# An encoder block in Strassen's form: product 1 of four gate groups by a second level, two groups at a time

## The chip, the cores and the metric

The kernel runs on one core of one Trainium2 chip. The metric is the device time of one execution in microseconds, the median of the runs; less is better. PE is the matrix engine, DVE the vector engine, ACT the scalar engine, POOL the GpSimd engine; SP issues the loads.

## The reference, cut to what matters

One layer on 1024 tokens of width 1024, all in float32:

```python
u = rms_norm(x, norm1_g)
q, k, v, cb, cc, ch, ga, gb = jnp.split(u @ w_in, split_pts, axis=-1)
...
y_a = neighbourhood_attention(q, k, v, rpb) @ w_attn_branch
y_b = short_gated_conv(cb, cc, ch, conv_w) @ w_conv_branch
merged = jax.nn.sigmoid(ga) * y_a + jax.nn.sigmoid(gb) * y_b
x = x + merged @ w_o
h = rms_norm(x, norm2_g) @ w_mlp_in
x = x + jnp.square(jax.nn.relu(h)) @ w_mlp_out
```

The change concerns `ga` and `gb`: 1024 tokens times 1024 inputs times 2 x 1024 gate columns of `w_in`.

## The kernel before

**Precision.** A float32 operand is scaled by a power of two and split into two float16 halves, high and low. A product takes three passes (high by high, low by high, high by low), so a product over 512 inputs, 128 output channels and 512 tokens is 4 x 3 = 12 matmuls of 512 columns.

**The gate stage.** Eight groups n = 0 to 7 follow one another. A group takes 128 channels of `ga` and the same of `gb`, and with the two halves of the inputs its weights are a matrix of 2 x 2 blocks (`ch.r`). It is computed by Strassen's scheme in Winograd's form, with seven products in place of eight: `SEVEN` gives for each product the form of the activations (0 to 6) and the form of the weights. Forms 0 to 3 of the activations are quarters or sums that lie in `UT`, 4 and 5 in space of `QD`, 6 in `s4T`; they are made once for all groups. Product 1 is the first quarter of the activations (inputs 0 to 511, tokens 0 to 511) by the first block of the weights, unsummed. `gate_units` (L1349) runs the products in the order 1, 6, 2, 4, 5, 7, 3 and joins them in the tile `sg` (two buffers in turn) by "posts" on DVE and ACT: product 1 is copied to `z[0]`, products 6 and 2 are added to it, `post7` and `post3` give the rest and the sigmoid. Then `branch_units` (L1463) runs four products of the attention's and the convolution's branch (two halves of the tokens each), whose posts multiply by the gates (L1489) and add (L1491) to `m`; `m_done` takes the largest value of `m` (L1344) and splits it into `mH` and `mL` (L1338, L1340).

**Preparing a group.** `prep_s(n + 1)` runs in the background of group n: `rows_scaled` multiplies the rows of the loaded weights by norm 1's gains (ACT, L1260), `forms_sum` squares them (ACT, L1269) and makes the four sums (POOL, L1274) in `gsum`, `sum_of` adds up the squares (L1240, L1241), `scale_of` sums over the partitions by a one-column matmul with `ones` (L201, in `all_sum`) and makes the scale from it in small DVE steps (L204, L435 to L442), and `forms_split` writes the float16 halves `w_s`, ACT the high one (L1294) and DVE the low one (L1290). The branch weights A and B are prepared by `Chunk.prep`: `largest` (L320 to L331), `all_sum`, `pow2`, split (L309 on ACT, L300 on DVE).

**The order.** The program's order is that of one Python run, and each engine takes its instructions in that order. A `unit` issues the matmuls of one product, then lets each generator in `hooks` make one step unless `hold` is set, then issues the posts of the product before it (`settle`), and then `steps` steps of the foreground (`fg`, that is `m_done`) in turn with `ticks` steps of the background (`bg`). A tick goes to the first generator of the background that isn't waiting. Generators wait by `apart` for a number of units, or of columns of matmul (`work`; 6144 is one product). `hold` is set while `w_s` is split. From group 1 on, `norms1` in `hooks` loads pieces of W1, into spare rows of `mH` and `mL` and a tile of its own, and sums their squares on ACT (L1386).

**PSUM.** Eight buffers of 512 columns, three of kind "d", three "s", two "o"; `anybank` goes round over the kinds as "dsodsods". The products, the branch halves and the one-column sums of the background all take theirs there. A new use of a buffer waits for the last reader of the old one.

In the MLP the same second level is in use before the change (`deep1`, `quarters`, `slices`): there, in groups 6 to 13, product 1 of two groups is done by seven smaller products; `w_d` are its weights, `quarter` and `a_d` its sums of the activations, `zt` its partial results.

## Time and profile before

| | us |
|---|---|
| median of 3 runs | 1194.14 (1193.83 to 1194.72) |
| the profiled execution | 1194.58 |
| its span in the trace | 1192.6 |
| PE busy in the span | 1185.4 |
| DVE busy | 959.0 |
| ACT busy | 769.3 |
| POOL busy | 410.5 |

The profiled execution took 2.0 us more than its span; these lie around what the trace shows. The gate stage runs from 297.6 us (product 1 of group 0) to 526.9 us, when the output projection begins. Times in rows are microseconds from the start of the span; a row of a timeline gives start, duration, engine, line, operation, output and inputs with their shapes, the count, and in brackets the idle time before it and what ended it. Matmuls overlap and their ends are modelled, so that the distance of two starts says more than a duration. Rows of a tile or line give the shortest, the median and the longest duration in ns.

### The profile page before, as it was taken

To read this page: it belongs to the slowest core of one execution; us is meant where nothing else is said; L and a number is where in the kernel's file an instruction comes from. 1 tells how busy PE (TensorE), PEld (TensorE's weight loads), DVE (VectorE), ACT (ScalarE), POOL (GpSimd) and SP (SyncE) were. 2 spreads that over 40 slices of the span, in tenths; PEclk is the share of its full clock that TensorE was granted. 3 is DMA by queue.
4 is the path that set the end of the run, shared out by engine and by line. 5 is a ranking of instruction groups with operands and counts; after the bars stand their busy time and mean duration, and the time that the engine had idled before them with its cause. 6 is when DMAs were issued, how large, how long until landed. Compare 5 with 4: busy or idle time off the path is not lost.

```text
span 1192.6 us, 17069 instructions
## 1 busy us (share of the span) xinstructions
PE 1185.4 (99%) x6291; PEld 581.3 (49%) x6291; DVE 959.0 (80%) x1666; ACT 769.3 (65%) x1192; POOL 410.5 (34%) x284
## 2 busy tenths in 40 slices
...
PEclk9999999999999999999999999999999999999999
...
GB/s 296 212 154 214 112 127 134 141 153 113 179 103 179 142 177 144 86 154 130 78 164 150 158 177 176 195 130 133 207 255 203 376 74 264 89 141 194 106 36 106
DMA packets 181283, 189.61 MB, mean 159 GB/s; under 512 B 138192, under 2 KB 138704, under 8 KB 177104
## 3 DMA queue, kind: packets, MB, share of 16 engines
...
## 4 chain that ended last, share of the span: by engine, by line
PE 57%; issue 6%; POOL 5%; DMA 3%; DVE 3%; ACT 2%; SPq 0%; POOLq 0%; DVEq 0%; ACTq 0%
PE ps_s L210 21%; PE ps_d L210 20%; PE ps_o L210 15%; DMA hs<-as 3%; POOL tsum L1671 3%; POOL as L1559 2%; PE ps_d L1158 1%; DVE w L1290 1%; DVE as L2009 1%; SPq L1149 0%; ACT raw L1662 0%; DMA raw<-in_weights 0%; PE ps_o L1122 0%; ACT as L1932 0%; DVE w_s L1290 0%
## 5 line engine op out<-in xcount | busy, mean ns | idle before, releaser
L210 PEld LDWEIGHTS <-ops 128*128 128x128 f16 x1356 | 132.5, 98 | 157.3
L210 PEld LDWEIGHTS <-w 128*128 128x128 f16 x1272 | 124.4, 98 | 127.1 <-issue 0.2
L1158 PE MATMUL ps_d<-uT,w_ws 128*128 128x512 f16 x528 | 123.7, 379 | 0.0
L210 PE MATMUL ps_d<-ops 128*128 128x512 f16 (+1 forms) x528 | 119.7, 377 | 0.0
L1559 POOL TENSOR_TENSOR as<-as 128x512 f32<-128x512 f32 x56 | 92.0, 1643 | 74.0 <-ACT as L1934 71.0
L210 PE MATMUL ps_s<-ops 128*128 128x512 f16 (+1 forms) x516 | 117.1, 377 | 0.0
L2186 ACT ACTIVATE ops<-hf,sc 128x2048 f16<-128x2048 f32 x26 | 52.0, 2000 | 86.0 <-PE ps_d L210 37.5
L210 PEld LDWEIGHTS <-w_s 128*128 128x128 f16 x672 | 65.1, 98 | 79.2 <-DVE w_s L1290 1.5
L210 PEld LDWEIGHTS <-uT 128*128 128x128 f16 x528 | 51.4, 98 | 62.4 <-issue 0.6
L1671 POOL TENSOR_TENSOR tsum<-raw 128x512 f32<-128x512 f32 x28 | 40.5, 1462 | 114.4 <-ACT raw L1662 114.4
L1158 PEld LDWEIGHTS <-w_ws 128*128 128x128 f16 x528 | 51.4, 98 | 54.2
L2188 DVE SCALAR_TENSOR_TENSOR ops<-hf,sc,ops 128x2048 f16<-128x2048 f32 x26 | 69.5, 2673 | 3.5 <-ACT ops L2186 3.5
L210 PE MATMUL ps_o<-ops 128*128 128x512 f16 x312 | 71.6, 379 | 0.0
L1274 POOL TENSOR_TENSOR gsum<-raw 128x512 f32<-128x512 f32 x14 | 18.6, 1341 | 125.4 <-ACT raw L1260 100.0
L210 PE MATMUL ps_d<-u2T,w 128*128 128x512 f16 (+1 forms) x276 | 58.2, 360 | 0.0
L1290 DVE SCALAR_TENSOR_TENSOR w<-tsum,sc,w 128x1024 f16<-128x1024 f32 x28 | 46.3, 1661 | 14.5 <-ACT w L1294 14.5
L210 PE MATMUL ps_s<-u2T,w 128*128 128x512 f16 (+1 forms) x252 | 54.0, 364 | 0.0
L1290 DVE SCALAR_TENSOR_TENSOR w<-raw,sc,w 128x1024 f16<-128x1024 f32 (+1 forms) x20 | 28.2, 1417 | 31.7 <-ACT w L1294 31.7
L1932 ACT ACTIVATE as<-as 128x2048 f32<-128x2048 f32 (+1 forms) x18 | 30.9, 1718 | 31.5 <-DVE as L2009 19.3
L1088 ACT ACTIVATE sz<-sz,sc 128x384 f32<-128x384 f32 (+1 forms) x64 | 37.2, 581 | 20.9 <-DVE sc L1079 13.7
L309 ACT ACTIVATE w_ws<-raw,sc 128x512 f16<-128x512 f32 (+1 forms) x64 | 37.2, 655 | 19.6 <-DVE sc L282 19.6
L210 PE MATMUL ps_s<-u2x,w 128*128 128x512 f16 (+1 forms) x228 | 48.5, 362 | 0.0
...
## 6 DMA issues: line engine op xcount, KB each, us to landing
...
```

The costliest lines, as they stand in the source:

```text
L210: T.matmul(ps, l, r, start=a, stop=b, skip_group_check=free)
L309: A.activation(self.parts[:, 0, f + o:f + o + m], self.raw[p][:, o:o + m], AF.Copy, scale=sc[:, c:c + 1])
L1088: A.activation(z, z, AF.Exp, scale=-1.0, bias=sc[:, d["mx"]], accum_out=sc[:, d["sm"]])
L1158: T.matmul(ps, l, r, start=a, stop=b)
L1274: G.tensor_tensor(t[:, o], a, b, op=OP.add)
L1290: V.scalar_tensor_tensor(o(1), w, sc[:, s], o(0), op0=OP.mult, op1=OP.subtract)
L1559: sub.tensor_tensor(z[o], z[a], z[b], op=op)
L1671: G.tensor_tensor(t[:, o], a, b, op=OP.add)
L1932: A.activation(v[:, 0:4], v[:, 0:4], AF.Relu)
L2009: add, less = (lambda o, a, b, op=op: V.tensor_tensor(o, a, b, op=op) for op in (OP.add, OP.subtract))
L2186: A.activation(P[:, 1, 0], hf, AF.Copy, scale=sc[:, Rs])
L2188: V.scalar_tensor_tensor(P[:, 1, 1], hf, sc[:, Rs], P[:, 1, 0], op0=OP.mult, op1=OP.subtract)
```

## The change

For the groups 2 and 3, and 4 and 5, product 1 of both is computed together: one product over 512 inputs, 2 x 128 channels and 512 tokens, seen as 2 x 2 blocks once more, becomes seven products over 256 inputs, 128 channels and 256 tokens (6 matmuls of 256 columns each). They run in three turns ("slices") of three, two and two products in front of and between the other six products of groups 2 and 4, into three buffers of PSUM that are kept over the turns; the second and third turn add to what the first has left there. The results for both groups go to `z[0]` of their tiles, and groups 3 and 5 begin with product 6.

- `quarters1`, a hook from group 0 on, makes the sums of the activations' first quarter on DVE and splits them (ACT, DVE) into spare rows of `mH` and `mL`.
- For each pair, group n's preparation also loads the first block of group n+1 (256 KB), scales and squares it, and makes the scales of both in one go; then four sums of 256 columns on DVE and five small pieces give the weights of the small products. The first block of the usual seven pieces is left out for both groups.
- The small products have a scale of their own, so products 6 and 2 are joined to them with a factor (`joined`).
- In groups 2 and 4, product 7's post is issued with product 3's; the order there is 5, 4, 7, 6, 2, 3 with the turns in between.
- Ticks: 9 per product in groups 2 and 4 and none at the turns, 6 in the other groups (before: 4, in group 7: 6), 3 per branch unit (before: 4).

```diff
@@ -253,7 +253,7 @@
...
-            self.split = False
+            self.split, self.q = False, None
...
@@ -1262,18 +1262,27 @@
 
     def forms_sum(ch, t, gap):
 
-        sm = cols_of("prep", 2)
+        pair = ch in cS.values() and ch is not cS[0] and ch in [cS[i] for i in PAIRS]
+        sm = cols_of("prep", 4 if pair else 2)
         for i in range(2):
             while len(ch.raw) <= i:
                 yield WAIT
...
+        if pair:
+            yield from pair_square([i for i in PAIRS if cS[i] is ch][0], sm)
         ch.r = [ch.raw[i].rearrange("p (n m) -> p n m", n=2) for i in range(2)]
         (w11, w12), (w21, w22) = ([r[:, 0], r[:, 1]] for r in ch.r)
         for o, a, b in ((0, w11, w12), (1, w12, w22), (2, t[:, 0], w22), (3, t[:, 2], w21)):
             G.tensor_tensor(t[:, o], a, b, op=OP.add)
         yield from apart(work[0], gap * 6144, work)
-        ch.sum = sum_of(sm)
+        if pair:
+            b, a = cols_of("prep", 2), ones[:, 132:134]
+            V.tensor_reduce(sc[:, b], sc[:, sm].rearrange("p (a b) -> p a b", a=2), axis=AX, op=OP.add)
+            V.tensor_copy(a, sc[:, b])
+            ch.sum = a, work[0]
+        else:
+            ch.sum = sum_of(sm)
         yield
 
     last_low = [-9]
@@ -1297,34 +1306,132 @@
 
     def forms_split(ch, t, s, P):
 
+        m = int(ch.q is not None)
+
         def then(n):
-            if n == 1 and ch is not c1[0]:
+            if n == 1 - m and ch is not c1[0]:
                 done[0] += 2
                 load_upto(done[0] + 5)
         r = ch.r
-        todo = [(0, 1, r[0][:, 0:1]), (1, 3, r[1]), (3, 5, t[:, 0:2]), (5, 7, t[:, 2:4])]
+        todo = [(0, 1, r[0][:, 0:1]), (1, 3, r[1]), (3, 5, t[:, 0:2]), (5, 7, t[:, 2:4])][m:]
         yield from parts([((lambda i, a=a, b=b: P[:, a:b, i]), w) for a, b, w in todo], s, then)
+
+    PAIRS = (2,4,)
+    gates, began, a16, sliced = {}, {}, [], set()
+
+    pieces_q = {}
+
+    def form_q(n):
+        v = [r.rearrange("p i (f c) -> p f i c", f=2) for r in pieces_q[n]]
+        return lambda a, b: v[a // 2][:, a % 2:a % 2 + b - a]
+
+    def quarters1():
+
+        z = [v.bitcast(F32) for v in (M[1][:, 1], M[1][:, 2], M[1][:, 3], M[0][:, 1], M[0][:, 2])]
+        rows4 = [v.rearrange("p (s k c) -> p s k c", s=2, k=2) for v in (M[0][:, 4], M[0][:, 5], M[1][:, 4], M[1][:, 5])]
+        for t in range(2):
+            for h in range(2):
+                hi, lo = (UT[:, i, 2 * h:2 * h + 2, 256 * t:256 * t + 256] for i in range(2))
+                V.tensor_tensor(z[2 * t + h].rearrange("p (k c) -> p k c", k=2), hi, lo, op=OP.add)
+                yield
+        for o, a, b, op in ((4, 0, 2, OP.subtract), (2, 2, 3, OP.subtract), (0, 2, 0, OP.subtract), (1, 1, 0, OP.add)):
+            V.tensor_tensor(z[o], z[a], z[b], op=op)
+            yield
+        prev = None
+        for f, i in enumerate((2, 0, 4, 1, None)):
+            if prev:
+                V.tensor_tensor(prev[1], prev[2], prev[0], op=OP.subtract)
+            if i is not None:
+                hi, lo = (rows4[f][:, w].rearrange("p k c -> p (k c)") for w in range(2))
+                A.activation(hi, z[i], AF.Copy)
+                prev = hi, lo, z[i]
+            yield
+        a16.extend(rows4)
+
+    def pair_load(n):
+
+        while n - 1 not in began or units[0] < began[n - 1] + 2:
+            yield WAIT
+        gates[n] = w3p.tile([128, 4, 512], F32, name="sg")
+        SP.dma_start(gates[n][:, 1], bass.AP(tensor=weights.tensor, offset=weights.offset + cS[n + 1].offs[0],
+                                             ap=[[1024, 128], [1, 512]]))
+
+    def pair_square(n, sm):
+
+        sg, ch = gates[n], cS[n]
+        for k in range(4):
+            v = sg[:, 1, 128 * k:128 * k + 128]
+            A.activation(v, v, AF.Copy, scale=sc[:, at(g1, 4 * 0 + k)])
+        for i, v in enumerate((sg[:, 1], ch.raw[0][:, 0:512])):
+            A.activation(sg[:, 2], v, AF.Square, accum_out=sc[:, at(sm, 2 + i)])
+        yield
+
+    def two_scales(am, n):
+
+        a, mark = am
+        yield from apart(mark, n * 6144, work)
+        b, s, inv = cols_of("prep", 2), cols_of("prep", 2), keep(2)
+        bk = anybank()
+        T.matmul(bk[:, 0:2], ones[:, 0:128], a, start=True, stop=True)
+        yield
+        V.tensor_scalar(sc[:, b], bk[:, 0:2], 1e-36, None, op0=OP.max)
+        yield
+        yield from pow2_half(b, 14, s, inv, 9)
+        return s, inv
+
+    def pair_split(n, s):
+
+        ch, sg, W = cS[n], gates[n], form_q(n)
+        x, y = ch.raw[0][:, 0:512], sg[:, 1]
+        d = sg[:, 2:4].rearrange("p a (h c) -> p (a h) c", h=2)
+        b11, b21, b12, b22 = x[:, :256], x[:, 256:], y[:, :256], y[:, 256:]
+        for o, a, b in ((0, b11, b12), (1, b12, b22), (2, d[:, 0], b22), (3, d[:, 2], b21)):
+            V.tensor_tensor(d[:, o], a, b, op=OP.add)
+        yield
+        two = lambda v: v.rearrange("p (h c) -> p h c", c=256)
+        yield from parts([((lambda i, a=a, b=b: W(a, b)[:, :, i]), w) for a, b, w in
+                          ((0, 2, two(x)), (2, 3, two(b22)), (3, 4, d[:, 0:1]), (4, 6, d[:, 1:3]), (6, 7, d[:, 3:4]))],
+                         s, lambda m: None)
+
+    def ratio(s, inv):
+        r = cols_of("prep", 1)
+        V.scalar_tensor_tensor(sc[:, r], sc[:, s], 2.0 ** 9, sc[:, inv], op0=OP.mult, op1=OP.mult)
+        return r
 
     def prep_s(n):
 
         ch = cS[n]
         t = w3p.tile([128, 4, 512], F32, name="gsum", bufs=1)
+        if n in PAIRS:
+            yield from pair_load(n)
         yield from rows_scaled(ch, g1)
-        yield from forms_sum(ch, t, 2 - 0 * (n != 3))
-        s, ch.inv = yield from scale_of(ch.sum, 9, 2 + 1*(n != 3), 0)
+        if n in PAIRS:
+            pass
+        yield from forms_sum(ch, t, (1+(n==2)) if n in PAIRS else 2)
+        s, ch.inv = yield from two_scales(ch.sum, 3) if n in PAIRS else scale_of(ch.sum, 9, 2 if n == 3 else 3, 0)
         hold[0] = True
-        while done[0] < ch.first:
+        while done[0] < ch.first or n - 1 in PAIRS and n - 1 not in sliced:
             yield WAIT
-        ch.P = wsp.tile([128, 7, 2, 512], F16, name="w16_s", tag="ws")
+        ch.P = wsp.tile([128, 8, 2, 512], F16, name="w16_s", tag="ws")
+        if n in PAIRS:
+            P, O = ch.P, cS[n - 1].P
+            pieces_q[n] = P[:, 0], P[:, 7], O[:, 7] if n == 2 else O[:, 0], M[0][:, 3].rearrange(
+                "p (i m) -> p i m", i=2) if n == 2 else O[:, 7]
+            yield from pair_split(n, at(s, 1))
+            ch.q, s, ch.inv = at(ch.inv, 1), at(s, 0), at(ch.inv, 0)
+        elif n - 1 in PAIRS:
+            ch.q = cS[n - 1].q
+        if ch.q:
+            ch.ratio = ratio(s, ch.q)
         yield from forms_split(ch, t, s, ch.P)
         ch.split = True
         hold[0] = False
 
     SEVEN = {1: (0, 0), 6: (4, 5), 5: (2, 3), 4: (3, 6), 2: (1, 1), 7: (5, 4), 3: (6, 2)}
 
-    def seven(P, act, c0, c1, posts, steps, ticks, order=(1, 6, 5, 4, 2, 7, 3)):
-
-        ps = {}
+    def seven(P, act, c0, c1, posts, steps, ticks, order=(1, 6, 5, 4, 2, 7, 3), ps=None):
+
+        ps = {} if ps is None else ps
         at_w = P if callable(P) else lambda w, i, k: P[:, w, i, k * 128:k * 128 + 128]
         for i in order:
             f, w = SEVEN[i]
@@ -1348,8 +1455,19 @@
 
     def gate_units(n, tail=None):
 
-        sg = w3p.tile([128, 4, 512], F32, name="sg")
+        began[n] = units[0]
+        sg = gates.pop(n, None)
+        if sg is None:
+            sg = w3p.tile([128, 4, 512], F32, name="sg")
         z = [sg[:, i] for i in range(4)]
+        q = cS[n].q is not None
+
+        def joined(o, i, ps):
+            if q:
+                V.scalar_tensor_tensor(z[o], z[0], sc[:, cS[n].ratio], ps[i], op0=OP.mult, op1=OP.add)
+            else:
+                V.tensor_tensor(z[o], ps[i], z[0], op=OP.add)
+
...
-        seven(cS[n].P, actS, 0, 512, {
-            1: lambda ps: A.activation(z[0], ps[1], AF.Copy),
-            6: lambda ps: V.tensor_tensor(z[1], ps[6], z[0], op=OP.add),
-            2: lambda ps: V.tensor_tensor(z[0], ps[2], z[0], op=OP.add),
-            7: post7, 3: post3}, 2, 4 if n < 7 else 6, (1, 6, 2, 4, 5, 7, 3))
+        posts = {1: lambda ps: A.activation(z[0], ps[1], AF.Copy), 6: lambda ps: joined(1, 6, ps),
+                 2: lambda ps: joined(0, 2, ps), 7: post7, 3: post3}
+        if n in PAIRS and LATE7:
+            posts[7], posts[3] = None, lambda ps: (post7(ps), post3(ps))
+        ticks = 9 if n in PAIRS else 6 if n < 7 else 6
+        if n in PAIRS:
+            ps, some = {}, gate_slices(n, z[0], z[3][:, 0:256])
+            for o, order in ORDERS:
+                for _ in range(o):
+                    next(some, None)
+                seven(cS[n].P, actS, 0, 512, posts, 2, ticks, order, ps)
+        else:
+            seven(cS[n].P, actS, 0, 512, posts, 2, ticks, (6, 2, 4, 5, 7, 3) if q else (1, 6, 2, 4, 5, 7, 3))
         return sg
+
+    ORDERS = ((1, (5, 4)), (1, (7,)), (1, (6, 2, 3)))
+    LATE7 = ORDERS[-1][1][-1] == 3 and 7 not in ORDERS[-1][1]
+
+    def gate_slices(n, za, y):
+
+        W, u, ps, zb = form_q(n), UT[:, :, 0:4, 0:512], {}, []
+        lo, hi = slice(0, 256), slice(256, 512)
+
+        def mms(k, i, first):
+            f, w = SEVEN[i]
+            act = lambda s, j: (u[:, s, j + 2 * (f & 1), 256 * (f >> 1):256 * (f >> 1) + 256] if f in (0, 1, 3)
+                                else a16[max(0, f - 3)][:, s, j])
+            m = [(W(w, w + 1)[:, 0, sw, j * 128:j * 128 + 128], act(sa, j)) for j in range(2) for sw, sa in PASSES]
+            return [(ps[k], l, r, first and o == 0, o == 5) for o, (l, r) in enumerate(m)]
+
+        def tt(o, x, y, op=OP.add):
+            V.tensor_tensor(o, x, y, op=op)
+
+        def p0():
+            gates[n + 1] = w3p.tile([128, 4, 512], F32, name="sg")
+            zb.append(gates[n + 1][:, 0])
+            A.activation(y, ps["a"], AF.Copy)
+            tt(zb[0][:, lo], ps["b"], y)
+
+        def p1():
+            tt(zb[0][:, hi], ps["b"], y)
+            tt(zb[0][:, hi], ps["c"], zb[0][:, hi], OP.subtract)
+
+        def p2():
+            A.activation(za[:, lo], ps["a"], AF.Copy)
+            tt(za[:, hi], ps["b"], y)
+            tt(zb[0][:, lo], ps["c"], zb[0][:, lo], OP.subtract)
+        for o, (three, post) in enumerate(zip((((1, "a"), (6, "b"), (5, "c")), ((2, "a"), (7, "b")),
+                                               ((4, "b"), (3, "c"))), (p0, p1, p2))):
+            both = []
+            for i, k in three:
+                if o == 0:
+                    ps[k] = anybank()[:, :256]
+                both += mms(k, i, o == 0)
+            unit(both, post, *ticks_s[o], True)
+            if o == 2:
+                sliced.add(n)
+            yield
+
+    ticks_s = ((0,0),(0,0),(0,0))
 
     def norms1(t, first):
 
@@ -1467,8 +1639,9 @@
             for half in range(2):
...
-                     lambda ps=ps, g=g, half=half, ch=ch: post(g, half, ps, sc[:, ch.inv]), 2, 4)
-
+                     lambda ps=ps, g=g, half=half, ch=ch: post(g, half, ps, sc[:, ch.inv]), 2, 3)
+
+    hooks.append(quarters1())
     for n in range(8):
         built(cS[n])
         if n < 7:
```

## The prediction

> **What bounds the kernel now.** I read the page's head first, then the stretches by window, then what PE waited for, then the timelines of PE and DVE around the gates.
>
> ```profile
> span 1192.6 us, 17069 instructions
> PE 1185.4 (99%) x6291; PEld 581.3 (49%) x6291; DVE 959.0 (80%) x1666; ACT 769.3 (65%) x1192; POOL 410.5 (34%) x284
> PEclk9999999999999999999999999999999999999999
> 336.70:364.80 28.10, 28.10 (x135) 12.76 (x134) 22.96 (x40) 15.78 (x25) 7.59 (x6) 1.00 0.35 113
> 355.45:376.25 20.80, 20.80 (x100) 9.48 (x99) 18.96 (x45) 12.59 (x25) 3.88 (x4) 1.00 0.54 186
> PE ps_d L210 <- DVE w_s L1290: 0.6, 1, 0.6
> ```
>
> PE fills the span at full granted clock. In the gate stage (297.5 to 527 us) its waits come to one line: 0.6 us, for weights of gate 1. So a column of matmul taken away there is time, as long as no new wait appears. The two window rows (PE, PEld, DVE, ACT, POOL busy) say what new waits could come from: DVE, 22.96 of 28.10 us over one gate, and 18.96 of 20.80 us (91%) over the first products of gate 2, which is just where the change puts its new work.
>
> ```profile
> 326.15 2.75 PE L210 MATMUL ps_o<-uT,w_s 128*128 128x512 f16 x12
> 328.74 0.59 PE L210 MATMUL ps_d<-qD,w_s 128*128 128x512 f16 x2
> 329.95 2.33 PE L210 MATMUL ps_d<-qD,w_s 128*128 128x512 f16 x10 [0.62 <-DVE w_s L1290]
> 332.12 2.75 PE L210 MATMUL ps_s<-uT,w_s 128*128 128x512 f16 x12
> 355.45 2.75 PE L210 MATMUL ps_s<-uT,w_s 128*128 128x512 f16 x12
> 718.91 0.82 PE L210 MATMUL ps_d<-u2T,w_d 128*128 128x256 f16 x6
> 720.88 2.75 PE L210 MATMUL ps_d<-u2T,w 128*128 128x512 f16 x12
> ```
>
> Read starts, not durations. A product of twelve 512-column matmuls takes 328.74 - 326.15 = 2.59 us (216 ns each). From 328.74 to 332.12 are 3.38 us for one product: PE lost 0.79 us to that wait. The MLP already runs the second-level products: 18 matmuls of 256 columns from 718.91 to 720.88, 1.97 us, 109 ns each.
>
> **What PE saves.** Per pair, two products (2 x 2.59 = 5.18 us) become seven small ones of 6 matmuls: 42 x 0.109 = 4.60 us. Two pairs save 2 x 0.58 = 1.2 us. This is the whole gain; with the old wait of 0.79 us gone too it would be 2.0 us.
>
> A rule of the Trainium skill speaks against it (TensorE: Matmul & The Clock Gate, Back-to-back issue gap): in a stream of load and matmul pairs it gives about 131 ns at 512 columns and 81 ns at 128, so halving the columns does not halve the time. An estimate from these figures for 256 is 98 ns, and the change would then cost 84 x 98 - 48 x 131 ns = 1.9 us on PE. Here the rows give 216 and 109 ns and decide; the same section's formula for the isolated gap, N/2.4 + 2.5 ns, fits them.
>
> **The sums of the activations (gate 0).** One step of `quarters1` is taken behind the matmuls of each unit: eight DVE sums behind the first eight units, one ACT copy behind the ninth; then the split of gate 1's weights holds the hooks back, and the remaining copies and differences come in gate 1.
>
> ```profile
> 311.31 0.69 DVE L1411 TENSOR_TENSOR sg<-ps_o,sg 128x512 f32<-128x512 f32 x1 [4.06 <-ACT sg L1451]
> 315.96 1.75 DVE L300 SCALAR_TENSOR_TENSOR w_wb<-raw,sc,w_wb 128x256 f16<-128x256 f32 x4 [2.40 <-ACT w_wb L309]
> 317.88 0.74 DVE L1489 SCALAR_TENSOR_TENSOR sg<-ps_o,sc,sg 128x512 f32<-128x512 f32 x1
> 318.54 0.68 DVE L1411 TENSOR_TENSOR sg<-ps_d,sg 128x512 f32<-128x512 f32 x1
> 320.74 0.75 DVE L1489 SCALAR_TENSOR_TENSOR sg<-ps_s,sc,sg 128x512 f32<-128x512 f32 x1 [0.79 <-ACT sg L1414]
> 327.42 2.48 DVE L1290 SCALAR_TENSOR_TENSOR w_s<-gsum,sc,w_s 128x1024 f16<-128x1024 f32 x2
> L1559 DVE TENSOR_TENSOR quarter<-quarter x4: 686/692/693, 661.9 to 664.1; 128x512 f32<-128x512 f32 x4
> L1745 DVE TENSOR_TENSOR quarter<-u2T x2: 1218/1220/1221, 656.6 to 658.4; 128x1024 f32<-128x1024 f16 x2
> ```
>
> A sum of 512 columns is 0.61 us from f16 (half of 1.22) and 0.69 us from f32. The first five find gaps: DVE idles 4.06 us before 311.31 and 2.40 us before 315.96, waiting for ACT. From 315.96 on DVE itself is the chain that ends in the wait of PE: the last pieces of gate 1's weights are done at 327.42 + 2.48 = 329.90, PE goes on at 329.95. The sixth and seventh sum fall between 317.88 (its place is by the order of the units: the post of the first branch half is settled in the sixth unit) and the posts at 318.54, with no gap to take them: 2 x 0.69 = 1.4 us on the chain. The eighth falls in front of 320.74, where DVE idled 0.79 us for a sigmoid, and costs nothing. So PE's wait in gate 1 grows from 0.79 to about 2.2 us: **+1.4 us**. Bounds: 0 if the sums come one unit earlier than I place them, 2.8 if POOL's sums slow them.
>
> **Preparing a pair (gates 1 and 3).** Added on ACT: four scalings and two squares of a half piece; on SP one 256 KB load per pair, behind which stand W1's loads for the norms, which are early. PE's sum of the squares is issued at the end of product 3 as before, so nothing is added there. Then come the small pieces:
>
> ```profile
> L1705 DVE TENSOR_TENSOR tsum<-raw x8: 409/413/1490, 699.6 to 807.8; 128x256 f32<-128x256 f32 x8
> L1294 ACT ACTIVATE w_d<-raw,sc x8: 494/602/712, 699.5 to 807.7; 128x512 f16<-128x512 f32 x4, 128x256 f16<-128x256 f32 x4
> L1290 DVE SCALAR_TENSOR_TENSOR w_d<-raw,sc,w_d x8: 474/610/746, 702.1 to 811.5; 128x512 f16<-128x512 f32 x4, 128x256 f16<-128x256 f32 x4
> L1290 DVE SCALAR_TENSOR_TENSOR w_s<-gsum,sc,w_s x14: 1279/1280/1283, 327.4 to 499.9; 128x1024 f16<-128x1024 f32 x14
> 345.34 0.15 DVE L204 TENSOR_SCALAR sc<-ps_s 128x1 f32<-128x1 f32 x1
> 345.78 0.68 DVE L1363 TENSOR_TENSOR sg<-ps_d,sg 128x512 f32<-128x512 f32 x1
> 346.49 2.00 ACT L1365 ACTIVATE sg<-sg,sc 128x2048 f32<-128x2048 f32 x1 [8.31 <-DVE sg L1363]
> L1489 DVE SCALAR_TENSOR_TENSOR sg<-ps_s,sc,sg x11: 739/745/751, 320.7 to 496.1; 128x512 f32<-128x512 f32 x11
> 361.64 0.69 DVE L1491 TENSOR_TENSOR m<-sg 128x512 f32<-128x512 f32 x1
> 354.05 1.22 DVE L320 TENSOR_REDUCE sc<-raw 128x4 f32<-128x1024 f32 x1
> ```
>
> In the time of the trace of before: scale from 345.34, done with its small steps and L1363 at 347.1; the sigmoid, 2.00 us, and the first piece of 512 columns, 0.71 us, end on ACT at 349.8. The four half sums (4 x 0.41) lie under the sigmoid. From 349.8 DVE does the five small pieces (2 x 0.75 + 3 x 0.47 = 2.9), the posts that come between them (3 x 0.745 + 0.69 = 2.9) and three pieces of 1.28 us: the last two end at 358.2 and 359.4, where before the split was over when L320 began, at 354.05. The small products begin at 355.45 and have what they need (354.1); product 5 needs its weights at 357.42 + 0.43, 0.3 us before they are there. DVE enters gate 2 about 4 us behind.
>
> **Inside a pair's gate.** Nine ticks a unit, so the splits of the branch weights and the scale of the next gate come in the first products; the posts of the small products come on top:
>
> ```profile
> L2009 DVE TENSOR_TENSOR zt<-ps_s,zt x6: 410/416/424, 721.5 to 834.6; 128x256 f32<-128x256 f32 x6
> L1344 DVE TENSOR_REDUCE sc<-m x7: 1220/1220/1221, 332.8 to 507.1; 128x1 f32<-128x1024 f32 x7
> 365.36 1.28 DVE L1340 SCALAR_TENSOR_TENSOR mL<-m,sc,mH 128x1024 f16<-128x1024 f32 x1 [0.35 <-ACT mH L1338]
> 370.84 1.68 DVE L300 SCALAR_TENSOR_TENSOR w_wb<-raw,sc,w_wb 128x256 f16<-128x256 f32 x4 [0.58 <-ACT w_wb L309]
> L1269 ACT ACTIVATE gsum<-raw x14: 1040/1052/1062, 311.2 to 471.7; 128x1024 f32<-128x1024 f32 x14
> ```
>
> By the order of issue DVE has, from the start of the three large pieces at 354.1 to the post of product 2: pieces 3.84, L320 twice 2.44, posts of gate 1's second branch 2.9, five posts of 256 columns 2.1, L1344 1.22, L1340 1.28, two branch splits 3.36, the posts of products 6 and 2 (now with a scalar, 0.745 each) 1.5, and some thirty steps of one to four columns at 0.15 us, 4.4: 23.0 us, to 377.1. (Starts lie up to 0.08 us closer than durations, 2.48 us for two pieces of 1.28: 1.4 us less over the queue; against it stand DVE's waits for the first scaled piece of each branch split, 0.58 us in the row of L300, twice, and 0.35 for L1338: I let them cancel.) PE, unhindered, has done its 4.60 us of small products and six products of 2.59 us at 355.45 + 20.1 = 375.6. What is next on PE is the first branch half; the buffers of PSUM go round over "d" (3), "s" (3) and "o" (2), and it falls on "o", where product 4 holds one until the late posts and product 2 the other until its post. So it waits for that post: **+1.4 us** in gate 2. Lower bound 0 (a piece less in the queue), upper 3 (each wait of DVE for ACT or a product is added).
>
> In gate 4 the round stands elsewhere (gate 3 has 11 buffers, not a multiple of 8), the branch falls on "d", where buffers are free; what is left is the third turn of the small products: it adds into buffers that the second turn's posts must have read, with one product (2.59 us) in between. In gate 2's times DVE has for it pieces 3.84, L320 2.44, posts 2.9, 0.4 and 0.8, L1344 1.22, steps 1.8: 13.4 us to 367.5, 0.8 less by the starts, 366.7; PE is there at 355.45 + 1.97 + 3 x 2.59 + 1.31 = 366.5. I take **+0.3 us** (0 to 1.0); in gate 2 the same 0.3 is part of the 1.4. DVE catches up in the branches, where it loses nothing.
>
> Gates 3 and 5 drop product 1 and start at product 6, whose weights are the last piece; but these pieces are issued with product 3 of the gate before, four branch units (10 us) ahead: nothing.
>
> **Sum.** -1.2 + 1.4 + 1.4 + 0.3 = **+1.9 us**. The profiled execution took 1194.58 us (span 1192.6 and 2.0 us around it), 0.44 above the median of 1194.14; that makes 1196.5 for it and **1196.0 us** as the median.
>
> **Rivals.** (1) All of it is hidden: -1.2 us, 1193.0, at best -2.0, 1192.2. For it: DVE idles 5.1 us in the gate of the first window row. Against: no gap between 317.88 and 320.0.
> (2) DVE bounds the pairs' gates, and it ends slower. Without the closer starts the third turn waits 1.0 us, 0.7 more than I took; and product 6 takes the buffer whose copy on ACT stands behind a square of W1's norms (1.05 us by the row of L1269). As soon as DVE is over 2.59 us behind at product 7, every further microsecond of its queue is PE's: 0.7 for the third turn and 0.6 for the copy (about half of such a square), twice, on top of the forecast: +1.9 + 2.6 = +4.5, 1198.6; with gate 2's upper bound 1200.2. For it: 91% in the second window row. Against: DVE's gaps around the sigmoid.
> (3) DVE is the bound all over. Then all that it gets is time: sums and splits of the activations 7.9 us, per pair 1.6 (half sums) + 1.4 (more pieces) + 2.1 (posts) + 0.2, in all 18.5: 1212.6. The trace speaks against it: PE's only loss in this stage was 0.79 us.
> The Trainium skill has this rule (Perfetto Trace Analysis, Identifying the Most-Contended Engine): matmul busy time is a bad measure, and the engine of the highest occupancy is the one to relieve; with loads at 49% and DVE at 80% that would be DVE. By the starts every 2.59 us the trace does not agree.
> (4) The change saves nothing, say because the small products run slower here than in the MLP: +3.1, 1197.2. The MLP's rows speak against it.
>
> **How the numbers follow.** Forecast 0.40, rival 1 0.18, rival 2 0.36, rival 3 0.02, rival 4 0.04. 0.2% is 2.4 us, about what a measurement of this kernel can tell from no change. Rival 1 stays within it even at its best (2.0), so faster has 0.02. The forecast's own range is 1193.8 to 1197.8 (+0 to +3.6); 0.33 of its 0.40 lie within, with all but 0.02 of rival 1 and 0.07 of rivals 2 and 4: same 0.56, slower 0.42. The range runs from just below rival 1 to rival 2's upper end: 1192.8 to 1200.2.
>
> **What would show it.** In the profile after: products of 256 columns at 109 ns in gates 2 and 4; PE's wait for w_s in gate 1 at about 2.2 us, with two sums between the first branch post and L1411; a wait of PE for a post of DVE at the first branch half of gate 2 and none in gate 4. The prediction is wrong if the wait in gate 1 stays at 0.8, if DVE reaches product 2's post before product 3 is done, or if PE waits anywhere else for over 1 us.

## The result, and the profile after

| | us |
|---|---|
| before, median | 1194.29 (1193.83 to 1194.72, 4 runs) |
| after, median | 1201.84 (1200.14 to 1202.14, 4 runs) |
| ratio | 1.0062, 95% interval 1.0051 to 1.0074 |
| the profiled execution after, and its span | 1200.14, 1198.0 |

The changed kernel is slower by 7.5 us, where 1.9 were forecast and 6.1 were the upper end. Head of the page after, and then the gate stage as one window (from product 1 of group 0 to the output projection; the columns are length, then busy time and instructions of PE, PEld, DVE, ACT, POOL, then granted clock, DMA share, GB/s), first of the kernel before, then of the one after:

```profile
span 1198.0 us, 17211 instructions
PE 1185.4 (99%) x6327; PEld 585.0 (49%) x6327; DVE 976.8 (82%) x1706; ACT 777.7 (65%) x1218; POOL 412.2 (34%) x284
```
```profile
297.60:526.73 229.13, 228.51 (x1075) 103.42 (x1072) 173.77 (x356) 145.28 (x242) 41.25 (x33) 1.00 0.43 136
```
```profile
296.63:531.82 235.19, 228.65 (x1112) 107.15 (x1109) 189.99 (x396) 153.89 (x268) 41.65 (x33) 1.00 0.42 134
355.20:380.07 24.87, 20.97 (x118) 11.27 (x117) 22.66 (x57) 16.48 (x34) 5.46 (x4) 1.00 0.50 176
```

The gate stage grew by 6.06 us, and DVE and ACT have 16.2 and 8.6 us more to do in it. The last row is gate 2 up to its first branch half: PE is idle for 3.9 of 24.9 us, DVE busy for 91%. What PE waited for in the gate stage after (waits in all, times, longest):

```profile
PE ps_s L210 <- DVE w_s L1299: 1.4, 1, 1.4
PE ps_d L210 <- DVE w_s L1299: 1.3, 1, 1.3
PE ps_o L210 <- DVE sg L1467: 1.2, 1, 1.2
PE ps_o L210 <- DVE sg L1517: 1.2, 2, 0.6
PE ps_s L210 <- ACT sg L1530: 1.0, 2, 0.5
```

Five lines stand where one stood (a sixth, for a one-column sum, has 0.2 us). Their places in gate 2, on PE's timeline (L1299 writes the low parts of weights, L1517 is a small turn's sum, L1530 ScalarE's copy of bank "a", L1467 the joining of products 6 and 2):

```profile
356.51 0.82 PE L210 MATMUL ps_d<-mH,w_s 128*128 128x256 f16 x6
357.16 0.59 PE L210 MATMUL ps_s<-uT,w_s 128*128 128x512 f16 x2
359.20 2.33 PE L210 MATMUL ps_s<-uT,w_s 128*128 128x512 f16 x10 [1.44 <-DVE w_s L1299]
...
367.86 0.17 PE L201 MATMUL ps_s<-ones 128*128 128x1 bf16 x1
368.17 0.16 PE L201 MATMUL ps_d<-ones 128*128 128x1 bf16 x1
368.93 0.81 PE L210 MATMUL ps_o<-uT,mH 128*128 128x256 f16 x6 [0.60 <-DVE sg L1517]
369.59 0.82 PE L210 MATMUL ps_d<-mL,w_s 128*128 128x256 f16 x6
370.90 2.75 PE L210 MATMUL ps_s<-qD,w_s 128*128 128x512 f16 x12 [0.50 <-ACT sg L1530]
...
376.11 2.75 PE L210 MATMUL ps_s<-s4T,w_s 128*128 128x512 f16 x12
380.07 2.10 PE L210 MATMUL ps_o<-qD,w_wa 128*128 128x512 f16 x9 [1.22 <-DVE sg L1467]
```

Taken as distances of two starts, less 216 ns for each matmul of 512 columns and 109 for one of 256, PE lost: 1.49 in gate 1; in gate 2 1.61 at product 5, 0.29 + 0.74 at the one-column sums and the third turn, 0.66 at product 6, 1.37 at the first branch half (A0); in gate 4 0.15, 0.36 + 0.74 and 0.67; in all 8.06. With the 0.78 of before gone and 1.17 us of matmuls saved, 229.13 - 0.78 - 1.17 + 8.06 = 235.24: the stage is accounted for. From its end to the last matmul are 661.48 us, 0.83 more than before. So 6.9 us are in these two stretches. The two profiled executions differ by less, 5.6 us (1194.58 and 1200.14): in the one after, the gates begin 0.97 us sooner and 0.5 us less lies behind the last matmul. It is the fastest of four (the other spans are 1.5 to 2.2 us longer), and no trace shows where the others lost it; over all profiles the gates begin between 296.6 and 298.3 us, though no edit touches what lies ahead of them. So the runs below are compared by stages and places, and by the time only beside that.

### The profile page after: what moved, and what is told of

Its sections match the earlier page's. It is cut to its first block, busy times and chain, and to the rows that moved or that the text cites. A ratio compares the mean times of both kernels' runs of the same rounds, so it can differ in the third digit from the quotient of the medians.

```text
span 1198.0 us, 17211 instructions
## 1 busy us (share of the span) xinstructions
PE 1185.4 (99%) x6327; PEld 585.0 (49%) x6327; DVE 976.8 (82%) x1706; ACT 777.7 (65%) x1218; POOL 412.2 (34%) x284
## 4 chain that ended last, share of the span: by engine, by line
PE 48%; DVE 9%; issue 7%; POOL 6%; ACT 5%; DMA 3%; POOLq 0%; DVEq 0%; ACTq 0%
PE ps_d L210 18%; PE ps_s L210 18%; PE ps_o L210 12%; POOL tsum L1844 3%; DMA hs<-as 3%; POOL as L1732 2%; DVE w_s L1299 2%; ACT raw L1260 1%; DVE w L1299 1%; DVE sc L320 1%; DVE sg L1662 1%; DVE P L1105 1%; DVE as L2182 0%; ACT w_s L1303 0%; ACT gsum L1270 0%
## 5 line engine op out<-in xcount | busy, mean ns | idle before, releaser
L210 PE MATMUL ps_s<-ops 128*128 128x512 f16 x480 | 110.1, 379 | 0.0
L210 PEld LDWEIGHTS <-w_s 128*128 128x128 f16 x702 | 68.0, 98 | 79.1 <-DVE w_s L1299 4.2
L210 PE MATMUL ps_o<-ops 128*128 128x512 f16 (+1 forms) x348 | 78.6, 375 | 0.0
L1299 DVE SCALAR_TENSOR_TENSOR w<-tsum,sc,w 128x1024 f16<-128x1024 f32 x28 | 47.1, 1691 | 14.5 <-ACT w L1303 14.5
L1299 DVE SCALAR_TENSOR_TENSOR w<-raw,sc,w 128x1024 f16<-128x1024 f32 (+1 forms) x20 | 28.2, 1416 | 31.7 <-ACT w L1303 31.7
L1844 POOL TENSOR_TENSOR tsum<-tsum,raw 128x512 f32<-128x512 f32 x28 | 47.6, 1699 | 1.1
```

The source lines that it names most:

```text
L210: T.matmul(ps, l, r, start=a, stop=b, skip_group_check=free)
L1299: V.scalar_tensor_tensor(o(1), w, sc[:, s], o(0), op0=OP.mult, op1=OP.subtract)
L1844: G.tensor_tensor(t[:, o], a, b, op=OP.add)
```

## The experiments

Losses of PE in us, worked out from starts as above. "Turn" is the third turn with the one-column sums before it; "MLP" is the stretch from the end of the gates to the last matmul.

| run | median | ratio, 95% interval | gate stage | gate 1 | gate 2: prod. 5 | turn | prod. 6 | halves | gate 4 | MLP |
|---|---|---|---|---|---|---|---|---|---|---|
| before | 1194.29 | | 229.13 | 0.78 | | | | | | 660.65 |
| after | 1201.84 | 1.0051 to 1.0074 | 235.19 | 1.49 | 1.61 | 1.03 | 0.66 | 1.37 | 1.92 | 661.48 |
| early sums | 1199.72 | 1.0032 to 1.0062 | 234.59 | 0.90 | 1.60 | 1.03 | 0.66 | 1.37 | 1.91 | 661.47 |
| pair 2 only | 1204.05 | 1.0070 to 1.0100 | 237.49 | 1.90 | 1.60 | 1.04 | 0.67 | 1.39 | 0 | 661.11 |
| bank shift | 1204.08 | 1.0062 to 1.0092 | 236.35 | 1.72 | 1.61 | 1.04 | 0.66 | 3.60 | 0.58 | 661.51 |
| late squares | 1198.26 | 1.0022 to 1.0045 | 233.60 | 2.21 + 1.70 | 0 | 0 | 0.57 | 1.39 | 0.58 | 661.49 |
| posts | 1201.91 | 1.0053 to 1.0081 | 235.89 | 2.18 | 1.63 | 1.05 | 0 | 2.05 | 1.89 | 661.55 |
| no low parts | 1197.78 | 1.0020 to 1.0044 | 233.71 | 2.21 | 0.55 | 1.04 | 0.67 | 1.38 | 0.26 | 661.47 |
| sums, squares, posts | 1198.80 | 1.0030 to 1.0055 | 232.75 | 0.46 | 0 | 1.26 | 0 | 2.05 | 1.89 | 661.53 |
| sums, squares, buffers | 1196.79 | 1.0012 to 1.0031 | 230.62 | 0.42 | 0 | 0 | 0.67 | 0 | 2.32 | 661.98 |
| the same and posts | 1197.34 | 1.0015 to 1.0033 | 232.23 | 0.93 | 0 | 1.25 | 0 | 0 | 2.93 | 661.50 |
| phase | 1200.46 | 1.0037 to 1.0062 | 235.49 | 1.78 | 1.61 | 1.04 | 0.67 | 1.38 | 1.92 | 660.85 |
| all | 1195.65 | 1.0003 to 1.0021 | 230.63 | 0.45 | 0 | 0 | 0 | 0 | 2.95 | 660.65 |
| all, new order | 1194.86 | 0.9996 to 1.0014 | 230.02 | 0.46 | 0 | 0 | 0 | 0 | 2.34 | 660.65 |
| and two sigmoids | 1193.80 | 0.9988 to 1.0007 | 228.92 | 0.88 | 0 | 0 | 0 | 0 | 0.91 | 660.69 |

**Early sums.** Two of the eight quarter sums behind each of the first four units.

```diff
                 V.tensor_tensor(z[2 * t + h].rearrange("p (k c) -> p k c", k=2), hi, lo, op=OP.add)
+            yield
...
+            V.tensor_tensor(z[o], z[a], z[b], op=op)
+            if n % 2:
                 yield
```

> The eight sums of the activations two to a unit, behind the first four units of gate 0, where DVE waits for ACT; copies and differences where they were. Theory (the sums on DVE's chain lengthen PE's wait in gate 1): that wait goes from 1.50 us in the changed kernel back to 0.8 (between 0.4 and 1.0), the other waits stay, and the time is 0.7 us below the changed kernel's, some 5.5 to 6.8 above the kernel before. Rival (ACT or the load of the weights sets it): the wait stays at 1.5 us.

Gate 1's wait fell to 0.90, nothing else moved. Over all profiles it is 1.5 to 2.2 with the sums as in the change (eight), 0.4 to 0.9 with two to a unit (eight), 0.8 and 1.1 without them: the sums do stand on the chain there, and cost about 1.0. The median fell by 2.1 us, of which the trace has 0.6: the two profiled executions are equal (1200.14 and 1200.16).

**One pair only.** Pair 4 alone, and pair 2 alone.

```diff
-    PAIRS = (2,4,)
+    PAIRS = (4,)
```

> Only groups 4 and 5 as a pair. Theory (each pair pays by its own waits): the waits of gate 4 stay near the 1.95 us of the changed kernel (third turn and product 6), gate 2 has none, gate 1 keeps 1.5: against the kernel before -0.6 + 0.7 + 1.95 = +2.1 us. Rival (DVE's backlog from gate 2 is carried on to gate 4): gate 4's waits fall below 1 us and the time is within 1 us of the kernel before.

> Only groups 2 and 3 as a pair. Theory: gate 2 keeps its 4.7 us of waits (product 5's weights 1.6, third turn and product 6 1.7, first branch half 1.4), gate 4 has none: -0.6 + 0.7 + 4.7 = +4.8 us against the kernel before. Rival (most of the loss is outside the pairs, by ticks or by the hooks): +2 us or less, or both single pairs over +5.

Pair 4 alone took 1215.26 us, a miss for every theory: gate 2, now with seven large products and 6 ticks each, met a one-column sum whose operand DVE had not made (5.8 us), and gate 4 lost over 11, in part by a slow clock (last section). Pair 2 alone kept gate 2's losses to 0.02, and got such a sum in gate 6 (3.18). The ticks fit the two pairs together, so these two runs do not price a pair.

**Bank shift.** Ahead of a gate's first buffer:

```diff
+        rc[0] += {2: 3, 3: 5}.get(n, 0)
         if n in PAIRS:
```

> The round of PSUM buffers moved by three places for gate 2 alone (and back by gate 3), so that it stands as in gate 4 and the first branch half takes a "d". Theory (the wait of 1.4 us there is for a buffer that the post of product 2 must free): it goes, no other comes, 1.4 us below the changed kernel. Rival (DVE is simply behind, and PE meets it at the next place): a wait of 1 us or more at the second branch half, at its second pair or at gate 3's first products, and less than 0.5 us won.

A0's wait went, and the next half, A1, waited 3.44 us for product 7's buffer, which is held until the late posts. So A0's wait is for a buffer; the shift put another half on one that is held longer. PE's timeline there, and the window behind it, whose clock (1.00) matters in the last section:

```profile
379.03 2.75 PE L210 MATMUL ps_d<-qD,w_wa 128*128 128x512 f16 x12
385.22 2.75 PE L210 MATMUL ps_s<-qD,w_wa 128*128 128x512 f16 x12 [3.44 <-DVE sg L1472]
```
```profile
385.22:390.00 4.78, 4.78 (x23) 2.17 (x23) 2.61 (x5) 2.09 (x2) 0.00 (x0) 1.00 0.55 216
```

**Late squares.** Why were product 5's weights 1.6 us late? The changed kernel in gate 1, rows of ACT, DVE and PE:

```profile
338.51 1.26 ACT L1364 ACTIVATE sg<-sg,sc 128x128 f32<-128x128 f32 x4
...
341.19 1.13 ACT L1445 ACTIVATE mH<-m,sc 128x1024 f16<-128x1024 f32 x1
342.36 1.28 DVE L1447 SCALAR_TENSOR_TENSOR mL<-m,sc,mH 128x1024 f16<-128x1024 f32 x1 [3.39 <-ACT mH L1445]
...
344.81 0.17 PE L1375 MATMUL ps_s<-ones 128*128 128x2 bf16 x1
...
347.07 0.15 DVE L1377 TENSOR_SCALAR sc<-ps_s 128x2 f32<-128x2 f32 x1
```

From 338.51 to 341.19 ACT scales and squares the pair's quarter; the split of gate 0's `m` stands behind it, and DVE idles 3.39 us for that split. Product 7's posts follow late, and the scale step (L1377) comes 2.26 us after PE's sum of the squares. Before it came 0.27 after (345.07 and 345.34). The edit puts the squares one unit later:

```diff
-        if pair:
-            yield from pair_square(...)
...
+        mark = work[0]
+        if pair:
+            yield from apart(units[0], 1)
+            for _ in range(2):
+                yield
+            yield from pair_square(...)
+        yield from apart(mark, gap * 6144, work)
```

> Edit: in preparing a pair, the two squares of the pair's quarter are put on ScalarE's queue one unit later, behind the split of m's high part, in place of ahead of it. In the changed kernel the split of gate 1's m stood at 341.19 behind 2.7 us of that work, VectorE idled 3.4 us for it, the posts of product 7 came late and the scale step stood at 347.07 where the kernel before had 345.34. Theory (VectorE's queue is late into gate 2 because of this): the scale step is back within 0.3 us of 345.3, product 5's wait of 1.6 us in gate 2 falls under 0.4, gate 2's wait at the first branch half falls from 1.4 to under 0.8 as well; the run is 1.5 to 2.5 us under the changed kernel, 1199.3 to 1200.3. Rival (the pair's pieces are late because VectorE's four sums and five low parts are simply longer than the time that is left): the scale step moves but the wait of 1.6 at product 5 stays above 1.1, and the time stays 1201.3 to 1202.3.

```profile
331.95 3.41 PE L210 MATMUL ps_d<-qD,w_s 128*128 128x512 f16 x10 [2.04 <-DVE w_s L1303]
...
348.76 0.17 PE L1379 MATMUL ps_s<-ones 128*128 128x2 bf16 x1
349.03 0.15 DVE L1381 TENSOR_SCALAR sc<-ps_s 128x2 f32<-128x2 f32 x1
```

The scale is 0.27 behind the sum again; product 5's wait is gone, and the third turn's in gate 2. A0's wait did not move, against what I expected, and the time fell by more than I expected. PE is also 2.4 us later out of gate 1 here (the 1.70 in the table is a slower clock, last section), which gave DVE time: in the runs below gate 1 loses 0.4 to 0.9, gate 2 is still free of both waits where the posts are as they were, but gate 4's come back. The clean comparison is the run early sums with the run sums, squares, buffers: neither stands long in gate 1, the buffers of the halves matter only behind these places, and product 5's wait goes from 1.60 to 0, the turn's from 1.03 to 0.12 (in the table a loss of so little is 0).

The turn's wait has a second source. Ahead of the one-column sums DVE multiplies two rows of four columns for each of the two branch weights (L102) and makes the sums' operand `ones` (L331). Behind the second `ones` stand three small steps and the sum of bank b (the first L1517), for which the turn waits. Rows of POOL and DVE in the changed kernel, and then the first L102 in the run sums, squares, buffers:

```profile
362.93 3.08 POOL L1277 TENSOR_TENSOR gsum<-gsum,raw 128x512 f32<-128x512 f32 x2
365.12 0.90 DVE L102 TENSOR_TENSOR sc<-sc 128x4 f32<-128x4 f32 x1
...
367.96 0.16 DVE L331 CAST ones<-sc 128x1 bf16<-128x1 f32 x1
...
368.47 0.41 DVE L1517 TENSOR_TENSOR sg<-ps_o,sg 128x256 f32<-128x256 f32 x1
```
```profile
363.38 0.15 DVE L102 TENSOR_TENSOR sc<-sc 128x4 f32<-128x4 f32 x1
```

L102 took 0.90 us in the one and 0.15 in the other; the long one ends when POOL's sum ends (366.0), the short one fell between two of POOL's sums. Leaving out the two runs with another course (turn later, pair 4 alone), the pairs' gates have 18 cases with a first L102 of 0.57 us or more, and there the turn and the sums ahead of it lost 1.03 to 1.53; in the 9 cases of 0.15 they lost 0.12 at most, once 0.75. So the late squares removed the turn's wait in two ways: DVE came sooner, and L102 missed POOL. An estimate of the second part is 0.90 - 0.15 = 0.75 of the 1.03; no run moves POOL's sums alone, so it isn't shown.

**Posts.** Bank a's copy behind the second turn; c read behind the first.

```diff
             tt(zb[0][:, lo], ps["b"], y)
+            tt(zb[0][:, hi], ps["c"], y, OP.subtract)
...
-            tt(zb[0][:, hi], ps["b"], y)
-            tt(zb[0][:, hi], ps["c"], zb[0][:, hi], OP.subtract)
+            tt(zb[0][:, hi], zb[0][:, hi], ps["b"], OP.subtract)
+            A.activation(za[:, lo], ps["a"], AF.Copy)
...
-            A.activation(za[:, lo], ps["a"], AF.Copy)
```

> Edit: the steps behind the three turns of small products are dealt out differently, the same sums: ScalarE's copy of the first bank goes behind the second turn (the bank is complete there) in place of the third, and the third bank is first read behind the first turn, so that behind the second turn only one sum on VectorE is left in place of two. Theory (the third turn waits for the second of two sums, 0.74 in each of gates 2 and 4, and product 6 for ScalarE's copy, 0.67 in each): the third turn's wait falls by the one sum, 0.3 to 0.5 each, product 6's to under 0.1 each; but the step behind the first turn grows by a sum, which the second turn may meet with up to 0.2; the run is 1.5 to 2.3 us under the changed kernel, 1199.5 to 1200.3. Rival (product 6's first half waits for VectorE's sums too, ScalarE's copy is only the last of several): 0.4 or more stays at product 6 in each gate, and the time is 1200.8 to 1201.5.

Product 6's wait went, and A0's rose from 1.37 to 2.05: DVE's queue ends when it did, so what PE gains ahead it gives back there. The third turn kept its wait, with one sum less behind the second turn. The expectation had the wrong sum: the turn waits for the first of the two, that of bank b (in the changed kernel it ends at 368.88 and the turn starts at 368.93), and the edit took the second from there.

**Early sums, late squares and posts together.**

> Edit: three edits together: the eight quarter sums dealt two to a unit into the first four units of gate 1, the pair's squares one unit later, and the posts of the small turns dealt out as in the run beside it. Theory (the waits are separate delays of the queues, each of which costs TensorE its own length): 0.6 + 1.6 + 2.0 off, and up to 1.0 more off the first branch half: 1196.5 to 1198.0, still above the kernel before, with what is left at gate 1 (0.9), the third turns (0.3 each) and the first branch half (0.5 to 1.4). Rival (VectorE is full over gates 2 and 4, so that what is taken from one wait comes back at the next): the sum of the lost time in the gates stays above 6 us, and the time above 1199.5.

The stage lost 5.65, and the time lies between the theories. Without the posts' edit (below) the third turn of gate 2 does not wait at all, so here that edit itself made the wait: with a sum more behind the first turn DVE comes to L102 later, and POOL holds it there for 0.95 us in place of 0.15. (The edit of the quarter sums is that of the run early sums, in gate 0.)

**Buffers.** The halves of gate 2 on kinds d, d, s, o; with early sums and late squares, then with the posts too.

```diff
-                ps = anybank()
+                ps = anybank({2: "ddso"}.get(n, [None] * 4)[2 * g + half])
```

> Edit: the early quarter sums and the late squares as before, the posts as in the changed kernel, and in gate 2 the four branch halves take buffers of the kinds d, d, s, o in place of o, d, s, d, so that none falls on a buffer that one of the late products holds. Theory (the first branch half's wait is one for the buffer of product 2, and no later work of VectorE is due there): the wait of 1.4 at A0 goes and nothing of over 0.3 takes its place among the four halves; the gate stage loses 4.0 to 5.0 us, the time is 1197.3 to 1198.5. Rival (VectorE's queue is what PE meets there, and the next half or gate 3 waits in its place): the halves of gate 2 or the first products of gate 3 wait 1.0 or more, and the time stays 1198.8 or more.

> Edit: all three edits of the run of that kind (early sums, late squares, posts dealt out anew), and the kinds d, d, s, o for gate 2's branch halves. Theory (that run's 2.05 at the first branch half goes, the rest stays: 0.5 in gate 1, 0.5 + 0.7 at the third turn of each pair, 0.6 in gate 4): the gate stage loses 3.3 to 3.9 us, the time is 1196.4 to 1197.4. Rival (as in the run beside it): a wait of 1.0 or more behind the first half, time 1198.4 or more.

```profile
373.62 2.75 PE L210 MATMUL ps_s<-s4T,w_s 128*128 128x512 f16 x12
376.21 5.34 PE L210 MATMUL ps_d<-qD,w_wa 128*128 128x512 f16 x24
```

No half waits, nor does gate 3; but gate 4, which PE now reaches sooner, loses 2.32 where late squares alone left 0.58 (L102 took 0.90 there, and 0.15 with late squares alone). The version without the posts' edit lost less: 3.40 against 5.10, where 3.3 to 3.9 was expected for the second.

**Turn later.** The third turn behind product 6, with that product's post put behind it, and other kinds for products 6 and 2 and the halves.

```diff
-    ORDERS = ((1, (5, 4)), (1, (7,)), (1, (6, 2, 3)))
+    ORDERS = ((1, (5, 4)), (1, (7, 6)), (1, (2, 3)))
...
+            posts[6], posts[2] = None, lambda ps: (joined(1, 6, ps), joined(0, 2, ps))
```

> Edit: as the run with buffers and posts, and the third turn of small products stands behind product 6 in place of ahead of it, with product 6's sum put behind it (it needs the finished first product); buffers for products 6 and 2 and the branch halves by kinds that are free then. Theory (the third turn and the one-column sums ahead of it wait 1.26 us in each pair because VectorE comes to the second turn's sum late in its queue; 2.59 us later it has): both waits go, no new one of over 0.5; the gate stage loses 0.8 to 1.6 us, and the time is 1193.8 to 1195.2, about that of the kernel before. Rival (VectorE is full from the splits of gate 1 to the halves of gate 2, so the sum of the waits comes back where the next result of VectorE is due): product 3, a half or gate 3's first product waits 1.0 or more in each pair, the gate stage loses 3 us or more, the time is 1196.4 or more.

1201.99 us. My choice of buffers spoiled it: products 2 and 6 took those of one-column sums that DVE reads late in its queue, with waits of 2.0 and 2.9 us (`DVE sc L204`). Whether the order could help stays open.

**No low parts.**

```diff
-                V.scalar_tensor_tensor(o(1), w, sc[:, s], o(0), op0=OP.mult, op1=OP.subtract)
+                if low:
+                    V.scalar_tensor_tensor(o(1), w, sc[:, s], o(0), op0=OP.mult, op1=OP.subtract)
...
-            m = [(W(w, w + 1)[:, 0, sw, j * 128:j * 128 + 128], act(sa, j)) for j in range(2) for sw, sa in PASSES]
+            m = [(W(w, w + 1)[:, 0, 0 * sw, j * 128:j * 128 + 128], act(sa, j)) for j in range(2) for sw, sa in PASSES]
```

This kernel leaves the low parts of the small products' weights out, so it doesn't compute the layer's value.

> Edit: the changed kernel with VectorE's five low parts of the small pieces left out in each pair (some 3.2 us of its queue by their rows of 0.47 and 0.75), and the small products read the high part of the weights twice in place of high and low; TensorE's work is the same, the value of the first product is not. Theory (the waits in gates 2 and 4 are VectorE's queue): the wait at product 5 of gate 2 falls from 1.6 to under 0.3, the one-column sums and the third turn in gate 2 from 1.0 to under 0.3, product 2's buffer frees earlier and A0's wait falls below 0.7; the time is 1198.3 to 1199.6. Rival (each wait has its own step: ScalarE's copies, the buffers, the ticks' order): product 5's wait falls, but the third turn keeps 0.6 or more and A0 1.0 or more, and the time is 1199.8 to 1201.0.

Product 5's wait fell to 0.55 and gate 4's to 0.26, but gate 2's third turn and A0 stayed to 0.01. In gate 4 the theory holds. In gate 2 the run can't tell it from the rival, for it hardly shortened the queue there. DVE, freed of the low parts, waits for ScalarE's high parts instead:

```profile
355.80 1.28 DVE L1300 SCALAR_TENSOR_TENSOR w_s<-raw,sc,w_s 128x1024 f16<-128x1024 f32 x1 [1.99 <-ACT w_s L1304]
```

From the end of its four sums to the end of the large pieces DVE took 10.19 us in the changed kernel and takes 9.13 here: 1.06 less, which is what product 5's wait fell by. PE still waits there, so all that follows runs from that wait as before. At 1197.78 the time lies under both ranges; the trace has 1.5 of those 4.1 us.

**Phase.** At the start of the MLP, in the changed kernel and in the kernel before:

```diff
     p3.close()
+    rc[0] += 4
```

> Edit: the changed kernel, with the counter that deals out accumulators (d, s, o, d, s, o, d, s) put on by 4 at the start of the MLP. The two pairs take 4 accumulators more than the kernel before, so that the MLP begins half a round further on; put on by 4 it begins as before. Theory (the order of the kinds sets which product of the MLP falls on an accumulator that is still held): the waits of 0.5 and 1.0 us, 266 and 303 us behind the gates, go, and the stretch from the end of the gates to the last matmul is 660.6 to 660.8 in place of 661.5; the time falls by 0.8, to 1200.7 to 1201.4. Rival (transfers or the activations' splits arrive otherwise because the gates end later): the two waits stay as they are, and so does the time.

> Edit: the kernel before, with the same counter put on by 4 at the start of the MLP, nothing else. Theory: the waits of 0.5 and 1.0 us appear in it, the stretch behind the gates is 661.4 to 661.6 in place of 660.65, and the time is 1194.7 to 1195.2, some 0.8 above the kernel before. Rival: neither changes.

What PE waited for in that stretch of the MLP, after and then with the counter put back:

```profile
PE ps_o L210 <- DVE as L2182: 0.8, 1, 0.8
PE ps_d L210 <- DVE as L2182: 0.3, 1, 0.3
```
```profile
PE ps_d L210 <- DVE zt L2183: 0.3, 1, 0.3
PE ps_s L210 <- DVE zt L2183: 0.2, 1, 0.2
```

The stretch is 660.85 in place of 661.48. In the kernel before, the same shift added only one of the two waits (0.62, 302 us behind the gates): 660.89 in place of 660.65, and 1194.67 us, ratio 1.0000 (0.9991 to 1.0009). So the counter's phase is a cause, worth 0.63 us in the one pair of runs and 0.24 in the other, where 0.8 was expected; how much depends on the phase and on the kernel.

**All, and a new order.** Early sums, late squares, buffers, phase, and ACT's copy of bank a behind the second turn; then also the order 3, 5, turn, 4, turn, 6, 2, 7.

```diff
-    ORDERS = ((1, (5, 4)), (1, (7,)), (1, (6, 2, 3)))
+    ORDERS = ((1, (3, 5)), (1, (4,)), (1, (6, 2, 7)))
```

> Edit: the run with early sums, late squares and the buffers d, d, s, o, and two more: ScalarE's copy of the first bank goes behind the second turn (VectorE's sums stay where they are), and the counter of accumulators is put on by 4 at the MLP. Theory (product 6 waits for that copy alone, as the bank's last reader; the MLP's waits are the counter's): product 6's 0.67 in each pair goes without a wait at the third turn of gate 2, the gate stage loses 2.0 to 2.4 us, the MLP 0.7: 1194.5 to 1195.3. Rival (product 6 meets VectorE's sums a little later, or the third turn waits as in the run that moved the sums too): the gate stage loses 3.2 or more, 1195.8 or more.

> Edit: as the run beside it with all edits, and the pairs' products in the order 3, 5, turn, 4, turn, 6, 2, 7 in place of 5, 4, turn, 7, turn, 6, 2, 3; product 3 reads pieces that are made first, so that those of products 5 and 4 have 2.6 us longer. Theory: the wait of 0.6 at gate 4's first large product goes, the third turn of gate 4 keeps 1.0 or a little less, the gate stage loses 1.0 to 1.9: 1193.4 to 1194.6, within 0.05% of the kernel before or a little under. Rival (VectorE is the bound of the stretch, so that TensorE catches it at the third turn): what goes at the first large product comes back at the one-column sums and the third turn (1.6 or more there), and the time is that of the run beside it, 1194.5 to 1195.3.

The copy alone took away product 6's wait (0.50 in the last row; in the run without that edit, the one with buffers, ACT's copy stood behind a square of the norms):

```profile
366.96 1.04 ACT L1566 ACTIVATE raw<-raw 128x1024 f32<-128x1024 f32 x1
368.00 0.36 ACT L1538 ACTIVATE sg<-ps_s 128x256 f32<-128x256 f32 x1
368.42 2.75 PE L210 MATMUL ps_s<-qD,w_s 128*128 128x512 f16 x12 [0.50 <-ACT sg L1538]
```

Gate 2 loses nothing of over 0.12 us any more. But the gate stage gained nothing by the copy: it loses 3.40 in both runs (230.62 and 230.63 us), for gate 4 rose from 2.32 to 2.95, with product 5 at 1.27 in place of 0.61 and a late branch half at 0.63. What the run won in the trace, 1.33, is the MLP's. In gate 4 the new order took these two away, and 0.82 came at the second turn and 0.48 more at the one-column sums: 2.34 in place of 2.95. The rival was the nearer: of 1.90 taken away 1.30 came back, where PE next met DVE's queue.

**Two sigmoids.** In gate 3 DVE idles 1.22 us for the high part of the pair's first piece, behind a sigmoid of 2.00 us. Half of that sigmoid is put behind two high parts.

```diff
+            if not tail and n + 1 in PAIRS:
+                c = 2
+                halves.append(lambda: A.activation(sg[:, 2:], sg[:, 2:], AF.Sigmoid, ...))
             A.activation(sg[:, :c], sg[:, :c], AF.Sigmoid, scale=sc[:, cS[n].inv])
...
+                while halves:
+                    halves.pop()()
```

> Edit: as the run with all edits and the new order, and the sigmoid of the gate ahead of each pair (128x2048, 2.0 us) in two halves, the second behind the first two high parts of the pair's pieces in place of ahead of them. Theory (VectorE idles 1.22 us for the high part of the first piece, and its queue has no idle time from there to gate 4's third turn): the low parts begin 0.8 to 1.0 us earlier and with them all that stands behind; gate 4's three waits fall from 2.3 to 1.2 to 1.5 us in all, the gate stage loses 1.7 to 2.0, 1193.6 to 1194.4, 0.5 to 1.0 under the run without this edit. Rival (the idle time comes back behind the second half of the sigmoid, or at the sum of four columns that waits for a slower engine): gate 4's waits keep 2.0 or more, and the time is 1194.6 or more.

DVE's first low part without and with it:

```profile
407.72 0.75 DVE L1303 SCALAR_TENSOR_TENSOR w_s<-raw,sc,w_s 128x512 f16<-128x512 f32 x1 [1.22 <-ACT w_s L1307]
```
```profile
406.31 0.75 DVE L1303 SCALAR_TENSOR_TENSOR w_s<-raw,sc,w_s 128x512 f16<-128x512 f32 x1 [0.37 <-ACT w_s L1307]
```

What PE still waits for in the whole gate stage with it:

```profile
PE ps_d L210 <- DVE w_s L1303: 0.7, 1, 0.7
PE ps_o L210 <- DVE sg L1529: 0.6, 1, 0.6
```

Gate 4 fell to 0.91 (L102 took 0.15 there, and 0.90 without the edit), and two waits are left. 1193.80 us against 1194.10 before in the same comparison, ratio 0.9997 (0.9988 to 1.0007): no difference can be told. The change's 1.17 us are earned and about as much is still lost.

## Why the prediction was right or wrong

- **What PE saves: right.** The small products start 0.65 us apart for six matmuls (356.51 to 357.16), as in the MLP.
- **Gate 1's sums: right in kind, size somewhat high.** 2.2 was forecast, 1.5 found in the changed kernel and up to 2.2 in others; early sums took it away. Of the two sums forecast behind the first branch post, one stood there (317.69) and the other ahead of it (316.43).
- **"Nothing is added there" (preparing a pair): wrong, the step that failed.** I had listed the scalings and squares on ACT, and asked only when PE issues the sum of the squares. What reads that sum stands on DVE behind a split that waits for ACT, and there the 2.7 us count. The scale step came 2.26 us after PE's sum in place of 0.27, and with it the whole queue of DVE into gate 2: product 5's 1.61, where I had 0.3 "late" and booked nothing, and the turn's 1.03 (late squares removed both).
- **Steps at 0.15 us: one term mis-sized.** I booked some thirty small steps at 0.15 each. One of them, L102, took 0.90 in gate 2 and 0.97 in gate 4, ahead of the turn; the trace of before already had it at 0.97 (355.84) and 0.71.
- **A0 in gate 2: the mechanism right, the size by luck** (1.4 forecast, 1.37 found, a buffer held by product 2; none in gate 4). Product 2's post ended at 380.02, where I had 377.1 (row below), and PE came there at 378.7, where I had 375.6: two errors of 3 us cancel, and my own figures give 1.5. Also, I had it take in the turn's wait, as if PE could lose in one place only. The waits ahead of it came on top, since DVE's queue slid with PE: 1.61 + 1.03 + 0.66 + 1.37 = 4.67.

```profile
379.28 0.74 DVE L1467 SCALAR_TENSOR_TENSOR sg<-sg,sc,ps_o 128x512 f32<-128x512 f32 x1
```

- **Gate 4: the size was off.** 0.3 forecast for the third turn, 1.10 found with the one-column sum ahead of it (L102's 0.97 stands in that queue); 0.67 at product 6, for ScalarE's copy, and 0.15 at product 5 weren't in the sum: 1.92 in all.
- **Rival 2 was the nearest.** Its third turn (1.0, found 0.74) and the copy behind a norm's square (0.6, found 0.66 and 0.67) are both there twice. It lacked product 5 and the MLP.
- **The MLP: not foreseen.** The pairs take four buffers more, which turns the order of kinds for all that follows (0.63 of the 0.83 by the run phase).
